# The recurrence's coefficients between the filters, its tables by eight pairs, its matrices by four groups, and the sums of tiles later

## The chip, the cores and the metric

The kernel runs on one core of a Trainium2 chip. The metric is the device time of one execution in microseconds (us). The core has TensorE (PE, with its weight loads shown apart as PEld), VectorE (DVE), ScalarE (ACT), GpSimd (POOL) and SyncE (SP), each with a queue of its own that is worked off in order, and 16 DMA engines.

## The reference

One layer of an encoder on two batches, a prompt of 1024 tokens and a sample of 256, with the same weights, all in float32:

```
x <- LN1(alpha*x + 0.5*SwiGLU_1(x))
x <- LN2(alpha*x + W_out[ RMS(S5(x)) ; RMS(Hyena(x)) ])
x <- LN3(alpha*x + 0.5*SwiGLU_2(x))
SwiGLU(x) = (silu(x @ w_gate) * (x @ w_up)) @ w_down       # 1024 -> 2816 -> 1024
S5:    ar, ai, bbr, bbi = discretize(lam, log_step, b)     # per direction, group and state
       h[l] = a * h[l-1] + bb u[l];  y = Re(c h) + d u     # 32 groups of 16 channels, 64 states, both directions
Hyena: k_f = rfft(filter);  z = gates[o] * (irfft(rfft(z) * k_f[o]) + bias[o] * z)
```

S5's coefficients depend on weights alone, as do Hyena's filters and their spectra. The kernel works them out at run time, beside the first SwiGLU.

## The kernel before, in words

**Precision.** Large products run as three products of float32 halves that PE takes in one pass: a helper `split` (L169 to L172) makes the high part on ACT (L171) and the low part on DVE (L172).

**Memory.** `Ctx.new` hands out buffers from 25 pieces of 2048 words per partition; a freed piece goes to the end of the list and is handed out again, and whoever writes it first waits until its last readers are through.

**Order.** The program is written by Python generators. `weave((gen, n), ...)` (L1567) always advances the generator whose yields so far, divided by its number n, are the smallest. The framework writes each engine's order when the program is built: what was emitted earlier has the higher priority, `high_priority(offset=...)` shifts it, and an instruction whose inputs are not expected yet is passed over. On the chip every engine then keeps that order.

**Stages.** The line of the weave tells what runs together:

- 0 to 527 us: `ffn` for four tiles (two of the sample, two of the prompt; 512 tokens) with `filter_spectra`, the filters of the sample and then of the prompt (L1722). Gate and up products are L298, down products L331. The weight loads of L281 and L314 are issued on SP shortly ahead of use.
- 527 to 1141 us: `ffn1_halves` for the prompt's other six tiles with `prep`, that is `s5_prep` and then `s5_mats` (L1723).
- then the in-projection with the scan (`s5`), which reads `scr["mat"]` and `scr["tab"]`; then Hyena with the sample's rest; from about 1925 us on the prompt's second SwiGLU.

**The six-tile SwiGLU.** `Blocks` holds seven operands made from x (two halves of the tokens, two halves of the features): "11", "21", "22" are blocks, "t1" to "t4" sums of blocks. `even` makes the first two, `odd` the others, with four subtractions on POOL (L1301), transposes on PE (L1308) and splits. `GateUp` makes seven operands of the weights, four of them sums (`sums`, L1363, on POOL in this SwiGLU, on DVE in the last one) which are split on ACT and DVE. `gated` then goes through 22 steps of 128 columns; each step has seven products of 12 matmuls (L1388), sums on DVE out of PSUM (L1409), a copy on ACT at its first product (L1421) and one store. `Down` (L1496) adds up the down products (L1541).

**The recurrence.** `s5_prep` (L432) works out the coefficients: some 130 DVE instructions on small tiles, most of them one after the other, thirteen PE instructions (nine transposes and products) and two Sin on ACT, with the loads of b (L507 to L509). It leaves `b23` (2 x 64 x 16 words per partition) and `tn` (7 x 2 x 32) in SBUF for `s5_mats` (L541). That makes tables first: for four pairs at a time seven levels of `cmul` (L421, six DVE instructions), each twice as wide as the last one, then copies on ACT and eight DMAs issued by ACT (L567) into `scr["tab"]`. Then the matrices: for two groups at a time six DVE products and sums (TT of L546), two transposes, two matmuls (L626) and two stores on SP.

The weaves and the buffers of the tables are

```
    weave((fa, 33), (filter_spectra((4, 5, 6, 7)), 155))
    weave((fb, 30), (prep((6, 7)), 165))
    ...
    c_, s_, n_, tm = K.ring(2, 4, 160), K.ring(2, 4, 160), K.ring(1, 4, 160), K.ring(1, 4, 64)
```

## Time and profile before

| | |
|---|---|
| median of 3 runs | 2615.12 us (2611.82 to 2616.24) |
| the profiled execution | 2612.26 us, its span 2610.5 us |
| instructions in the span | 32833 |
| PE busy | 2499.4 us (96%), 12605 matmuls |
| DVE busy | 1934.4 us (74%) |
| ACT, POOL busy | 865.8 us (33%), 213.3 us (8%) |
| mean granted PE clock | 0.987 |

Busy time is the time in which an engine had an instruction in work. Matmuls are pipelined and overlap, so a busy PE may still run below its rate; the number of matmuls in a stretch and the granted clock tell more. "Idle before" is what an engine stood still ahead of an instruction, with the engine and line that ended the wait. A line can be a helper's: L171 and L172 are all splits, L424 to L429 all of `cmul`.

### The profile page before, as it was taken

The page shows a single profiled execution, that of the slowest core. Times are in us where ns is not written, and L with a number is a line of the kernel's source. Part 1 is how long each engine was busy: PE and PEld are TensorE (multiplying, and loading weights), DVE is VectorE, ACT ScalarE, POOL GpSimd, SP SyncE. Part 2 cuts the span into 40 slices and gives each one's busy share as a digit, 9 for nine tenths or more (in the row PEclk, how much of TensorE's full clock was granted, in tenths as well). Part 3 has the DMA queues.
Part 4 walks back from the last instruction along what each step waited for, and adds up shares of the span by engine and source line. Part 5 has one row for each costly group of instructions (what it writes and reads, how often), then busy time and mean ns, then how long its engine had stood idle before and what let it go on. Part 6 is the DMA issues. An engine that isn't in the chain of part 4 may idle for free.

```text
span 2610.5 us, 32833 instructions
## 1 busy us (share of the span) xinstructions
PE 2499.4 (96%) x12605; PEld 2124.7 (81%) x12605; DVE 1934.4 (74%) x3153; ACT 865.8 (33%) x1315; POOL 213.3 (8%) x158
## 2 busy tenths in 40 slices
PE   8999999978989899999999999999989999999998
PEld 6777788878879888888888878999768888888887
DVE  6777777598997887466896978798886656556437
ACT  5443443333334342123444413333332222223200
POOL 0000000243233200010000000000230000000001
PEclk9999999989999999999999999999989999999999
DMA  6322332452545475355556654565332322235311
GB/s 196 118 88 85 100 107 89 137 130 68 148 144 141 138 234 154 92 163 146 158 171 190 222 204 147 161 194 154 121 130 89 93 77 82 88 131 200 118 44 65
DMA packets 359156, 346.90 MB, mean 133 GB/s; under 512 B 42220, under 2 KB 309125, under 8 KB 358230
## 3 DMA queue, kind: packets, MB, share of 16 engines
q1 hardware_dynamic: 323446, 326.44, 39.9%
q10 hardware_dynamic: 35552, 18.36, 2.6%
q8 instruction: 99, 1.62, 0.3%
q14 instruction: 59, 0.48, 0.1%
HBM read 261.37 MB, written 83.11 MB: 132 GB/s over the span
## 4 chain that ended last, share of the span: by engine, by line
PE 68%; DVE 20%; DMA 4%; issue 3%; POOL 2%; ACT 2%; SPq 0%; ACTq 0%; DVEq 0%; POOLq 0%
PE banks L1388 19%; PE banks L1541 14%; PE banks L298 12%; PE banks L331 5%; DVE s L172 4%; PE banks L860 4%; DVE s L930 3%; PE banks L777 3%; PE banks L1242 3%; PE banks L1064 2%; POOL s L1363 1%; ACT s L171 1%; DVE s L245 1%; DMA s<-in_ffn_w_gate_dram 1%; DVE s L1409 1%
## 5 line engine op out<-in xcount | busy, mean ns | idle before, releaser
L1388 PE MATMUL banks<-s,s 128*128 128x512 f32 (+1 forms) x3500 | 768.7, 371 | 26.2 <-DVE s L1409 17.0
L171 ACT ACTIVATE s<-s 128x1024 fp32r<-128x1024 f32 (+4 forms) x533 | 478.9, 915 | 845.5 <-PE banks L1541 132.9
L1388 PEld LDWEIGHTS banks<-s,s 128*128 128x128 f32 x3500 | 647.0, 191 | 106.4 <-DVE s L1409 19.2
L172 DVE TENSOR_TENSOR s<-s,s 128x1024 fp32r<-128x1024 f32 (+4 forms) x533 | 570.1, 1081 | 181.4 <-ACT s L171 170.0
L298 PE MATMUL banks<-s,s 128*128 128x512 f32 (+1 forms) x2112 | 400.5, 342 | 2.4 <-ACT s L171 1.2
L1541 PE MATMUL banks<-s,s 128*128 128x512 f32 x1232 | 386.8, 392 | 0.1
L298 PEld LDWEIGHTS banks<-s,s 128*128 128x128 f32 x2112 | 325.4, 191 | 53.0 <-issue 10.3
L1541 PEld LDWEIGHTS banks<-s,s 128*128 128x128 f32 x1232 | 230.4, 188 | 46.6 <-DVE s L172 0.6
L1541 PE MATMUL banks<-s 128*128 128x512 f32 x616 | 241.2, 392 | 0.0
L860 PE MATMUL banks<-s,s 128*128 128x512 f32 (+1 forms) x1152 | 237.6, 360 | 0.0
L1409 DVE TENSOR_TENSOR s<-banks,s 128x384 f32<-128x384 f32 (+1 forms) x220 | 136.0, 618 | 111.9 <-PE banks L1388 110.9
L860 PEld LDWEIGHTS banks<-s,s 128*128 128x128 f32 x1152 | 188.3, 189 | 28.2 <-DVE s L172 0.4
L331 PE MATMUL banks<-s,s 128*128 128x512 f32 x792 | 200.8, 396 | 4.1 <-ACT s L171 2.3
L1547 DVE TENSOR_TENSOR s<-banks,s 128x512 f32<-128x512 f32 x140 | 95.8, 688 | 134.3 <-PE banks L1541 134.2
L230 POOL TENSOR_TENSOR cst<-cst 128x1 f32<-128x1 f32 (+2 forms) x38 | 47.8, 1258 | 1618.0 <-DVE cst L229 1618.0
L331 PEld LDWEIGHTS banks<-s,s 128*128 128x128 f32 x792 | 144.9, 188 | 35.7 <-ACT s L171 2.7
L1541 PEld LDWEIGHTS banks<-s 128*128 128x128 f32 x616 | 115.8, 188 | 22.7
L1242 PE MATMUL banks<-s,s 128*128 128x512 f32 x480 | 124.7, 407 | 4.1 <-ACT s L171 1.6
L1242 PEld LDWEIGHTS banks<-s,s 128*128 128x128 f32 x480 | 89.3, 190 | 23.4 <-ACT s L171 2.0
L679 DVE TENSOR_TENSOR s<-banks,s 128x512 f32<-128x512 f32 (+2 forms) x112 | 59.1, 550 | 44.5 <-ACT s L796 20.4
L171 ACT ACTIVATE s<-banks 128x512 fp32r<-128x512 f32 x81 | 46.8, 596 | 131.1 <-PE banks L221 68.0
L777 PE MATMUL banks<-s,s 128*128 128x256 f32 x624 | 89.7, 285 | 0.0
(218 smaller groups left out, 2634.9 us busy)
## 6 DMA issues: line engine op xcount, KB each, us to landing
s<-in_ffn_w_gate_dram SPq DMA_DIRECT2D x88, 512.0 KB
s<-in_ffn_w_up_dram SPq DMA_DIRECT2D x88, 512.0 KB
s<-in_ffn_w_down_dram SPq DMA_DIRECT2D x88, 512.0 KB
scr_h<-s SPq DMA_DIRECT2D x22, 512.0 KB
s<-scr_h SPq DMA_DIRECT2D x22, 512.0 KB
scr_tab<-s ACTq DMA_DIRECT2D x64, 160.0 KB
s<-scr_mat SPq DMA_DIRECT2D x16, 640.0 KB
s<-scr_tab SPq DMA_DIRECT2D x16, 640.0 KB
```

The costliest lines, as they stand in the source:

```text
L171: K.nc.scalar.activation(out=hi, in_=src, func=AF.Copy)
L172: K.nc.vector.tensor_tensor(out=lo, in0=src, in1=hi.bitcast(F32), op=ALU.subtract)
L298: nc.tensor.matmul(pss[-1][c], lhsT=w[:, wv, d], rhs=xT.parts[k][c].at(d), start=(d == 0 and wv == 0 and k == 0), stop=(d == 7 and wv == 1))
L331: nc.tensor.matmul(ps, lhsT=h[s // 4][:, a, s % 4 * 128:(s % 4 + 1) * 128], rhs=w[:, b, dh * 512:(dh + 1) * 512], start=(n == 0), stop=(n ...
L777: nc.tensor.matmul(ps, lhsT=F[kt][a].v[:, s, i], rhs=b.v[:, s], start=(n == 0), stop=(n == 3 * NT // R - 1))
L860: nc.tensor.matmul(p, lhsT=w[:, wv, d], rhs=xT[nm].parts[k][c].at(d), start=(d == 0 and wv == 0 and k == 0), stop=(d == 7 and wv == 1))
L930: TT = lambda o, a, b, op: V.tensor_tensor(out=o, in0=a, in1=b, op=op)
L1242: nc.tensor.matmul(ps, lhsT=y[s // per][a].v[:, k, ts], rhs=W[k].v[:, b, dh * 512:dh * 512 + 512], start=(k == 0 and a == 0 and b == 0), s ...
L1388: self.K.nc.tensor.matmul(ps, lhsT=w[i][:, d], rhs=x[k][:, d], start=first and m == 0, stop=m == len(todo) - 1, skip_group_check=True)
L1409: TT = lambda o, a, b: V.tensor_tensor(out=o, in0=a, in1=b, op=ALU.add)
L1541: nc.tensor.matmul(ps, lhsT=p[a].v[:, o:o + 128], rhs=p[b].v[:, dh * 512:dh * 512 + 512], start=m == 0, stop=m == len(todo) - 1)
L1547: nc.vector.tensor_tensor(out=xv, in0=ps, in1=xv, op=ALU.add)
```

## The change

- `filter_spectra` runs the sample's filters, then `s5_prep`, then the prompt's filters. `s5_prep` stores its two results in DRAM (`scr["b"]`, `scr["turn"]`), and `s5_mats` loads them again.
- `s5_mats` makes the tables for eight pairs at a time with one set of buffers, and yields after every level; the matrices for four groups at a time.
- `Blocks` gets its buffers in two goes. `ffn1_halves` makes all even blocks first, and the four sums of the first weights and all odd blocks in `begin`, behind the first two products. Of the down weights two instead of three loads are issued ahead.
- `gated` issues the first product of step 1 ahead of the sixth of step 0, in both SwiGLUs that use it; the four buffers for c1, u2, u3 become two for c1 and one each for u2 and u3.
- The weaves' numbers change.

```diff
@@ s5_prep
-    keep.update(b=b23, turn=tn)
+    for k, b in (("b", b23), ("turn", tn)):
+        nc.sync.dma_start(out=keep[k], in_=b.v)
+        b.free()
     yield 4
@@ s5_mats
-    er, ei = keep["turn"].v[:, :, 0], keep["turn"].v[:, :, 1]
-    c_, s_, n_, tm = K.ring(2, 4, 160), K.ring(2, 4, 160), K.ring(1, 4, 160), K.ring(1, 4, 64)
-    for j in range(0, 32, 4):
+    turn, bs = K.new(7, 2, 32), K.new(2, 64, 16)
+    nc.sync.dma_start(out=turn.v, in_=keep["turn"])
+    nc.sync.dma_start(out=bs.v, in_=keep["b"])
+    er, ei = turn.v[:, :, 0], turn.v[:, :, 1]
+    c_, s_, n_, tm = (K.ring(1, 8, n) for n in (160, 160, 160, 64))
+    for j in range(0, 32, 8):
         d, q = divmod(j, 16)
...
             cmul(K, c[:, :, n:2 * n], s[:, :, n:2 * n], c[:, :, 0:n], s[:, :, 0:n],
-                 bc(er[:, lev, j:j + 4], 2, n), bc(ei[:, lev, j:j + 4], 2, n), t[:, :, 0:n])
+                 bc(er[:, lev, j:j + 8], 2, n), bc(ei[:, lev, j:j + 8], 2, n), t[:, :, 0:n])
+            yield 1.5
...
-                nc.scalar.dma_start(out=scr["tab"][half * 64:half * 64 + 64, q:q + 4, v, gg, d], in_=src[gg * 64:gg * 64 + 64])
-        yield 7
+                nc.scalar.dma_start(out=scr["tab"][half * 64:half * 64 + 64, q:q + 8, v, gg, d], in_=src[gg * 64:gg * 64 + 64])
+        yield 1.5
...
-    inj, injt = K.ring(1, 2, 8, 16), K.ring(2, 2, 128)
-    outm, tmp = K.ring(1, 2, 9, 16), K.ring(1, 2, 9, 16)
+    inj, injt = K.ring(1, 4, 8, 16), K.ring(2, 4, 128)
+    outm, tmp = K.ring(1, 4, 9, 16), K.ring(1, 4, 9, 16)
...
-            for q in range(0, 8, 2):
+            for q in range(0, 8, 4):
...
-                yield 2
+                yield 4
@@ Blocks
-        self.b = {n: (K.newr(4, self.width), K.newr(4, self.width)) for n in self.NAMES}
+        self.b = {}
         self.tmp = K.ring(1, 4, 512) if tmp else None
+
+    def make(self, names):
+        for n in names:
+            self.b[n] = self.K.newr(4, self.width), self.K.newr(4, self.width)
@@ gated
-    tmp, hb = K.ring(4, T), K.ring(1, 2, T)
+    cr, tmp, hb = K.ring(2, T), K.new(2, T), K.ring(1, 2, T)
...
     G.parts(1)
+    p1(1)
     p6(0)
...
-        if ft < END:
+        if 0 < ft < END:
             p1(ft + 1)
@@ emit
     def filter_spectra(ids):
         FC = filt_consts(K, A)
-        for nm in NAMES[::-1]:
-            yield from filters(K, A, nm, FC, scr, ids, {})
+        yield from filters(K, A, "sample", FC, scr, ids, {})
+        yield from s5_prep(K, A, scr, Banks(K, ids[-2:]))
+        yield from filters(K, A, "prompt", FC, scr, ids, {})
...
         X = Blocks(K, N // 2, False)
-        for j in range(N // 2):
-            x = K.new(2, D)
+        X.make(X.NAMES[0:2])
+        xs = [K.new(2, D) for _ in range(N // 2)]
+        for j, x in enumerate(xs):
             for i in range(2):
                 nc.sync.dma_start(out=x.v[:, i], in_=src[:, first + 2 * j + i])
             X.even(x.v, j, tb)
-            if j < N // 2 - 1:
-                X.odd(x.v, j, tb)
-                x.free()
         G = GateUp(K, g("ffn1_w_gate"), g("ffn1_w_up"), True)
         G.load()
         yield 0.01
         G.parts(0)
-        G.sums(0, 0)
-        G.sums(0, 1)
+        X.make(X.NAMES[2:])
         G.load()
 
         def begin():
-            X.odd(x.v, N // 2 - 1, tb)
-            x.free()
+            G.sums(0, 0)
+            G.sums(0, 1)
+            for j, x in enumerate(xs):
+                X.odd(x.v, j, tb)
+                x.free()
...
-            if n in (1, 2, 5):
+            if n in (1, 2):
                 dn.load()
...
-    weave((fa, 33), (filter_spectra((4, 5, 6, 7)), 155))
-    weave((fb, 30), (prep((6, 7)), 165))
+    weave((fa, 33), (filter_spectra((4, 5, 6, 7)), 183))
+    weave((fb, 33), (s5_mats(K, A, scr, scr, dict(prep=(6, 7))), 115))
```

## Rows read from the trace of the kernel before

**Rows 1.** The page's first part: busy us (share) xinstructions of each engine.

```profile
PE 2499.4 (96%) x12605; PEld 2124.7 (81%) x12605; DVE 1934.4 (74%) x3153; ACT 865.8 (33%) x1315; POOL 213.3 (8%) x158
```

**Rows 2.** Stretches: us; busy of PE, PEld, DVE, ACT, POOL; PEclk, DMA share, GB/s.

```profile
30.00:467.00 437.00, 429.00 (x2099) 339.04 (x2098) 329.97 (x465) 191.35 (x235) 0.00 (x0) 1.00 0.33 105
467.00:527.00 60.00, 59.99 (x296) 49.10 (x295) 37.96 (x56) 21.22 (x32) 16.12 (x12) 1.00 0.44 145
527.00:560.00 33.00, 23.27 (x116) 20.84 (x115) 31.87 (x56) 12.02 (x22) 21.04 (x14) 0.90 0.68 193
560.00:640.00 80.00, 71.31 (x380) 68.99 (x379) 69.09 (x181) 25.28 (x55) 22.37 (x16) 0.91 0.24 58
640.00:796.00 156.00, 134.95 (x719) 130.79 (x717) 147.00 (x477) 52.48 (x108) 47.51 (x34) 0.95 0.51 145
796.00:829.00 33.00, 30.39 (x173) 30.00 (x174) 19.58 (x34) 12.47 (x25) 14.03 (x10) 1.00 0.56 151
829.00:935.00 106.00, 96.38 (x576) 91.92 (x575) 92.06 (x169) 42.30 (x93) 24.84 (x18) 1.00 0.51 155
935.00:1141.00 206.00, 204.33 (x981) 168.09 (x980) 153.47 (x250) 52.44 (x74) 7.54 (x5) 1.00 0.49 151
1436.00:1951.00 515.00, 492.78 (x2744) 428.10 (x2743) 432.57 (x591) 167.97 (x262) 46.84 (x36) 0.98 0.52 169
1951.00:2360.00 409.00, 408.87 (x1803) 337.51 (x1802) 245.18 (x323) 118.06 (x150) 0.00 (x0) 1.00 0.31 99
```

**Rows 3.** Groups by line, 527 to 935 (busy, mean ns | idle before, releasers).

```profile
L1388 PE MATMUL banks<-s,s 128*128 128x384 f32 x1634 | 339.6, 347 | 22.5 <-DVE s L1409 17.0 <-DVE s L172 5.5
...
L172 DVE TENSOR_TENSOR s<-s,s 128x512 fp32r<-128x512 f32 x156 | 126.9, 829 | 26.8 <-ACT s L171 26.2
```

**Rows 4.** Timeline of PE, 553 to 576: start, us, what [idle before].

```profile
556.65 8.10 PE L1388 MATMUL banks<-s,s 128*128 128x384 f32 x45 [1.72 <-DVE s L1409]
...
574.67 1.65 PE L1388 MATMUL banks<-s,s 128*128 128x384 f32 x4 [3.67 <-DVE s L1409]
```

**Rows 5.** Waits, 527 to 935: who for whom, us in total, times, longest.

```profile
POOL s L1363 <- DVE s L172: 202.0, 35, 15.0
ACT s L171 <- POOL s L1363: 109.2, 51, 5.6
```

**Rows 6.** Line L1421, 790 to 835: ns min/median/max, first and last start.

```profile
L1421 ACT COPY s<-banks x3: 461/463/468, 796.4 to 829.5; 128x384 f32<-128x384 f32 x3
```

**Rows 7.** Busy us of DVE on line L546 alone, by stretch.

```profile
527.00:935.00 408.00, 50.43 (x94) 0.95 0.47 135
935.00:1050.00 115.00, 41.41 (x103) 1.00 0.58 182
```

**Rows 8.** Busy us by stretch while the loads of b run.

```profile
575.00:580.00 5.00, 5.00 (x17) 5.00 (x17) 4.95 (x24) 0.63 (x1) 0.42 (x1) 0.50 0.80 93
```

**Rows 9.** Groups of DVE by line and shape, 640 to 796.

```profile
L426 DVE TENSOR_TENSOR s<-s,s 128x4 f32<-128x4 f32 x8 | 4.5, 558 | 0.2
...
L425 DVE TENSOR_TENSOR s<-s,s 128x256 f32<-128x256 f32 x8 | 3.3, 416 | 0.0
...
L425 DVE TENSOR_TENSOR s<-s,s 128x128 f32<-128x128 f32 x8 | 2.3, 283 | 0.0
```

**Rows 10.** Timeline of DVE: two short instructions in a row.

```profile
594.17 0.21 DVE L424 TENSOR_TENSOR cst<-cst 128x64 f32<-128x64 f32 x1
594.30 0.21 DVE L425 TENSOR_TENSOR s<-cst 128x64 f32<-128x64 f32 x1
```

**Rows 11.** Line L567, all of it: ns min/median/max, first and last start.

```profile
L567 ACTq DMA_DIRECT2D scr_tab<-s x64: 582/637/1577, 654.5 to 804.4; - x64
```

**Rows 12.** Timeline of PE at the start of the last SwiGLU.

```profile
1937.49 2.92 PE L1388 MATMUL banks<-s,s 128*128 128x512 f32 x6 [2.26 <-DVE s L172]
```

**Rows 13.** The page's third part: ACT's DMA queue (packets, MB, share).

```profile
q10 hardware_dynamic: 35552, 18.36, 2.6%
```

**Rows 14.** Line L546, all of it: what DVE waited for (us, times).

```profile
  DMA scr_mat<-s: 1.2, 2
```

More of the change, by code (lines that the diff above doesn't have):

```diff
@@ L566, in s5_mats @@
             for gg in range(2):
-                nc.scalar.dma_start(out=scr["tab"][half * 64:half * 64 + 64, q:q + 4, v, gg, d], in_=src[gg * 64:gg * 64 + 64])
-        yield 7
-    for r in (c_, s_, n_, tm, keep["turn"]):
+                nc.scalar.dma_start(out=scr["tab"][half * 64:half * 64 + 64, q:q + 8, v, gg, d], in_=src[gg * 64:gg * 64 + 64])
+        yield 1.5
+    for r in (c_, s_, n_, tm, turn):
         r.free()
     banks, bank1 = Banks(K, cfg["prep"][:-1]), Banks(K, cfg["prep"][-1:])
-    bb, bb1 = keep["b"].v[:, 0], keep["b"].v[:, 1]
+    bb, bb1 = bs.v[:, 0], bs.v[:, 1]
     pwr, pwi = K.pw[:, 0], K.pw[:, 1]
     cin, cst, gw = K.ring(2, 2, 2, 64), K.ring(1, 2, 8, 16), K.ring(2, 15, 16)
-    inj, injt = K.ring(1, 2, 8, 16), K.ring(2, 2, 128)
-    outm, tmp = K.ring(1, 2, 9, 16), K.ring(1, 2, 9, 16)
+    inj, injt = K.ring(1, 4, 8, 16), K.ring(2, 4, 128)
+    outm, tmp = K.ring(1, 4, 9, 16), K.ring(1, 4, 9, 16)
     nc.sync.dma_start(out=K.dcol, in_=g("ssm_d").rearrange("(b g) h -> (g h) b", b=4))
@@ L595, in s5_mats @@
             kp = bank1.get(8, 16)
-            for q in range(0, 8, 2):
+            for q in range(0, 8, 4):
                 dg, gg = d * 32 + b * 8 + q, b * 8 + q
                 def powers(lo, hi, rev):
-                    r, i = (p[:, lo:hi, dg:dg + 2] for p in (pwr, pwi))
+                    r, i = (p[:, lo:hi, dg:dg + 4] for p in (pwr, pwi))
                     if rev:
@@ L606, in s5_mats @@
                 r, i = powers(0, 8, d == 0)
-                TT(iv, bc(bb[:, dg:dg + 2], 2, 8), r, ALU.mult)
-                TT(tv, bc(bb1[:, dg:dg + 2], 2, 8), i, ALU.mult)
+                TT(iv, bc(bb[:, dg:dg + 4], 2, 8), r, ALU.mult)
+                TT(tv, bc(bb1[:, dg:dg + 4], 2, 8), i, ALU.mult)
                 TT(iv, iv, tv, ALU.add)
                 it = injt.get()
-                ps = banks.get(2, 128)
+                ps = banks.get(4, 128)
                 with K.tc.high_priority(offset=-50):
-                    for j in range(2):
+                    for j in range(4):
                         nc.tensor.transpose(ps[:, j], iv[:, j].rearrange("p a b -> p (a b)"), K.ident)
                 nc.scalar.copy(out=it, in_=ps)
-                nc.sync.dma_start(out=scr["mat"][:, gg:gg + 2, d], in_=it)
+                nc.sync.dma_start(out=scr["mat"][:, gg:gg + 4, d], in_=it)
                 ov, tv = outm.get(), tmp.get()
                 r, i = powers(0, 9, d == 1)
-                TT(ov, bc(cs_[:, 0, q:q + 2], 2, 9), r, ALU.mult)
-                TT(tv, bc(cs_[:, 1, q:q + 2], 2, 9), i, ALU.mult)
+                TT(ov, bc(cs_[:, 0, q:q + 4], 2, 9), r, ALU.mult)
+                TT(tv, bc(cs_[:, 1, q:q + 4], 2, 9), i, ALU.mult)
                 TT(ov, ov, tv, ALU.add)
-                nc.sync.dma_start(out=scr["mat"][:, gg:gg + 2, 2 + d], in_=ov[:, :, 1 - d:9 - d].rearrange("p g t h -> p g (t h)"))
+                nc.sync.dma_start(out=scr["mat"][:, gg:gg + 4, 2 + d], in_=ov[:, :, 1 - d:9 - d].rearrange("p g t h -> p g (t h)"))
                 with K.tc.high_priority(offset=-100):
-                    for j in range(2):
+                    for j in range(4):
                         nc.tensor.matmul(kp[:, q + j], lhsT=ov[:, j, d:d + 8].rearrange("p t h -> p (t h)"), rhs=bb[:, dg + j],
                                          start=True, stop=True)
-                yield 2
+                yield 4
             nc.scalar.copy(out=K.kev, in_=kp.rearrange("p a b -> p (a b)"))
@@ L641, in s5_mats @@
                               in_=gv[:, 7 - s:15 - s].rearrange("p t h -> p (t h)"))
-    for r in (cin, cst, gw, inj, injt, outm, tmp, keep["b"]):
+    for r in (cin, cst, gw, inj, injt, outm, tmp, bs):
         r.free()
@@ L1418, in p1 @@
     def p1(ft):
-        st[ft] = s = {"ps": [K.ps[:, b * 512:b * 512 + T] for b in ids[ft % 2]], "c1": tmp.get()}
+        st[ft] = s = {"ps": [K.ps[:, b * 512:b * 512 + T] for b in ids[ft % 2]], "c1": cr.get()}
         product(ft, 1, 0, True)
@@ L1431, in p6 @@
         product(ft, 6, 1, True)
-        s["u2"] = tmp.get()
+        s["u2"] = tmp.v[:, 0]
         TT(s["u2"], s["ps"][1], s["c1"])
@@ L1440, in p7 @@
         product(ft, 7, 1, False)
-        s["u3"] = tmp.get()
+        s["u3"] = tmp.v[:, 1]
         TT(s["u3"], s["ps"][1], s["c1"])
@@ L1491, in gated @@
             yield 0.6
-    for r in [tmp, hb] + G.sv:
+    for r in [cr, tmp, hb] + G.sv:
         r.free()
@@ L1642, in filter_spectra @@
         FC = filt_consts(K, A)
-        for nm in NAMES[::-1]:
-            yield from filters(K, A, nm, FC, scr, ids, {})
-    keep, out, x1T = {}, {}, {}
+        yield from filters(K, A, "sample", FC, scr, ids, {})
+        yield from s5_prep(K, A, scr, Banks(K, ids[-2:]))
+        yield from filters(K, A, "prompt", FC, scr, ids, {})
+    out, x1T = {}, {}
     gi = mix_in(K, A, x1T, out, scr, dict(win=((0, 1, 2), (3,)), wtr=(4,)))
-    def prep(ids):
-        yield from s5_prep(K, A, keep, Banks(K, ids))
-        yield from s5_mats(K, A, keep, scr, dict(prep=ids))
     def to_mix():
@@ L1852, in prompt @@
                             X = Blocks(K, 4, True)
+                            X.make(X.NAMES)
                         turn(j - 1)
```

2 lines of the change are left out of this document (1 added, 1 removed).

## The prediction

> **What bounds the kernel now.** I read the page's first lines, then the busy times by stretch, then the groups of lines and the waits of the one stretch that stands out. The page says PE 96% busy and would leave nothing to gain [rows 1]. The stretches say otherwise [rows 2]. In 1951 to 2360, the last SwiGLU, PE has no idle time and DVE is at 60%. In 30 to 467, the first SwiGLU woven with the filters, PE idles 8.0 of 437 us with DVE at 75.5%. In 527 to 935, the gate and up products of six tiles woven with the whole preparation of the recurrence, PE is busy 356.3 of 408 us (the five stretches from 527 on), so 51.7 idle, and its clock is granted at 0.90, 0.91 and 0.95 in the first three, which is 3.3 + 7.2 + 7.8 = 18.3 us more: 70 us lost, 17%. DVE is busy there 359.6 of 408, 88%. The same rows give a scale of DVE share against PE idle: 75.5% with 1.8%, 84.0% with 4.3% (1436 to 1951), 86.8% with 9.1%, 94.2% with 13.5%.
>
> The groups show how DVE reaches PE: PE waits mostly for the sums of L1409 [rows 3], single waits up to 3.67 us [rows 4]. A second loop runs beside it: POOL's sums wait 202 us for DVE's splits, and ACT's splits 109 us for POOL [rows 5]. At full clock 45 products in a row take 8.10 us [rows 4], some 0.175 us each, so one of the 22 steps (84 products) needs 14.7 us of PE, 323 for all and about 328 with the small matmuls, against 408.
>
> **Part 1, the coefficients move between the filters.** The stretch 796 to 829 holds exactly two steps (L1421 opens each; it comes at both ends and once between [rows 6]) and none of the preparation's arithmetic: DVE 19.6 us, so 9.8 a step, 215 for 22. The other 145 us of the 360 are 50 of L546 [rows 7], in 640 to 796 some 57 of tables (147 less 9.2 steps of 9.8), 3 more of them ahead of 640, and so about 35 for the coefficients. These 35 leave. In the stage from 30 on POOL does nothing; without it I take 28 us (25 to 34, the present size). There DVE has 330 of 437; with 28 more the share nears 82%, and by the scale the PE idle share goes from 1.8 to about 3.7%: 429 / 0.963 = 445.5, **+8.5 us**. The weave stretches the filters from 28.1 to 28.9 of 33 units, so part falls into 467 to 527, where DVE is at 63%.
>
> The step's other instructions move too. While b is loaded (L507, L508) the DMA engines are 80% busy for only 93 GB/s [rows 8]. Beside them now stand the SwiGLU's weight loads on SP, which are needed soon after they land, at a DMA share of 0.33. Cost 0 to 10 us (the 10 us of the busy stretch); I take 3, as those engines have room. The 13 PE instructions and two Sin calls: 1.5. The two new stores on SP wait for the last operation of the step, and the weight loads issued after them wait behind; that is within the same 0 to 10. The two loads back, 1.2 MB, take some 8 us at 145 GB/s; the first cmul waits for them, the first two steps' weights have been issued before: 0 (0 to 3). Stage one together: **+13 us** (3 to 40).
>
> **Part 2, tables by eight pairs.** 336 cmul instructions become 168 of twice the width. A 128-element one takes 283 ns, a 256-element one 416 [rows 9], so 128 elements cost 133 and 150 ns are fixed; of two in a row the second starts 0.13 us after the first, which lasts 0.21 [rows 10], so 70 to 150 ns of each removed one are really saved: 12 to 25 us, I take 18. The width of 512 has a near row: L172 at 829 ns mean with POOL's sums beside it [rows 3].
>
> The SBUF lock speaks against longer instructions. One group of 128x4 instructions has a mean of 558 ns, twice that of a 128x128 group [rows 9], where POOL is busy 47.5 of 156 us [rows 2]. The Trainium skill ("SBUF — State Buffer", Who interferes with whom) says that a VectorE operation with two SBUF inputs and a GpSimd operation exclude each other for a whole instruction. By that rule fewer instructions meet POOL, but POOL stands behind each for longer; the rows bear out the first half, and no row here shows the second apart.
>
> If POOL's 88 sums each waited 0.27 us more (150 + 4 x 133 = 682 instead of 416 ns), it would be 23 us of an engine that is busy 30% of this stretch (124 of 408); half of that on the path is 12, none is 0. I take 0 and keep 12 for the range.
>
> **Part 3, matrices by four groups.** 192 products and sums become 96; 92 us over the whole (50 in the stretch, 41 behind it [rows 7]) less 7 to 14, so 81. Where they fall changes: the tables take 48 of 115 units against 33, 13.8 steps, and the matrices 18.4 more, of which 8.2, 45%, lie within the 22 steps (before 58%). 37 us instead of 50: 13 saved. In 935 to 1141 there are then 44 instead of 41 on a DVE that is 74% busy under a PE that idles 1.7 us: 0 (-1 to +3). The 40 copies and DMA issues of 0.64 us [rows 11] fewer are ACT's, which is under half busy.
>
> **Part 4, sums later.** At the start POOL has 12 subtractions of the odd blocks and 4 sums. Now ten of the subtractions are over by 527 (POOL 16.1 in 467 to 527), and PE idles 9.7 of the next 33 us. If all wait for the start, the sixth product needs 15 POOL operations of 1.4 us, 21 us, over which PE has three products (6.3) and 84 transposes (9): 6 us worse. If POOL starts early, as now, the third product fills 2.1 us and the tail is lighter: 6 better. I take 0, inside the next sum. In the last SwiGLU the same product (12 matmuls of 0.227, by 409 us for 1803 in its stretch [rows 2]; 2.7 us) moves into a gap where PE waits 2.26 us [rows 12]: **-2** (-4 to +2). One weight load fewer ahead of the down products: a row of 36 products lasts 9.4 us (206 / 22) and its 0.9 MB land in 6 at 151 GB/s, so two ahead are enough: 0 (to +6, once).
>
> **The sum.** DVE from 527 on: 360 - 35 - 18 - 13 = 294. At 82% that is 358 us, 30 over PE's 328. By the scale about 4% idle (14 us), and the rest for the clock after waits and for small gaps, which now take 28 of the 80. So 408 becomes 358, **-50**; 16 us a step and 6 for the start. Bounds: -75 when PE has its 328 and 5, -25 when steps stay near 17. Together -50 + 13 - 2 = -39 on the profiled execution's 2612.3: 2573. That execution lies 2.8 below the median of the runs, 2615.1, so the forecast is 2576.
>
> **Rivals.** (A) *One set of tables.* c and s have one buffer each instead of two, so DVE's memset at L553 waits until the set before has landed, and DVE works in order: L1409 and PE stand behind it. Price: eight issues of 0.64 us, 5, and 2.6 MB; ACT's queue moved 18.36 MB in 2.6% of the span [rows 13], 9.7 us for a set alone, 19 if half the engines are taken; 7 us pass anyway (1.5 of 115 units at 16 us a step). 9 to 18, three times, say 41: 2576 + 41 = **2617**. It decides if the built order puts the memset before the landing. Against it: the single buffer of -s and of the matrices exists already, and DVE waited 1.2 us in all for the matrices' stores [rows 14]. (B) *Slower: stage one becomes what the second is.* The filters' arithmetic gets denser (160 units in 28.9 instead of 132 in 28.1) and DVE's order there has PE's matmuls behind it. If 30 to 467 loses the 17% that 527 to 935 lost, 429 / 0.83 = 517, +80 in place of +13: 2576 + 67 = **2643**. It decides from a loss of 11%, where 429 / 0.89 = 482 is 45 us more and eats the gain; on the scale that is a DVE share near 90%, and I get 82. (C) *The loop and not DVE's load.* In 796 to 829 DVE is at 59%, and PE still idles 7.9%: split, sum, split, sum depend on each other across three engines. If steps stay at 17.5 the gain is 15: 2615 - 15 + 13 - 2 = **2611**.
>
> **How the numbers follow.** Forecast 0.72 (2545 to 2604), A 0.09, B 0.11, C 0.08. What can be told from no change is 0.2%, 5 us. Faster: 0.72 and a third of A and of C, 0.78. Same: the rest of A and C, nearly, 0.09. Slower: B and a little of A and C, 0.13. The range goes from the forecast's best end with a lighter start, 2540, to A, 2617; B lies outside.
>
> **What would show it.** From 527 on: DVE 290 to 300 us, clock back at 1.00, steps of about 16 us, 168 cmul lines the widest of 0.68 us. From 30 to 467: L436 and L507 in it, PE idle under 20 us. DVE waiting at L553 for scr_tab would be A; a DVE share of 90% before 467, B; DVE below 80% with steps of 17.5, C. I am wrong if stage one gives back over 40, or if DVE's relief leaves the waits at L1409 as long as they are.

## The result, and the profile of the changed kernel

The changed kernel takes 2594.4 us (median, 2592.7 to 2595.0) against 2614.3, a ratio of 0.9923 (95% interval 0.9906 to 0.9940). The forecast was 2576: the sign is right, and half of the expected 39 us came. The profiled execution has a span of 2592.3 us.

The page's first part, as [rows 1]: DVE has 34 us and 280 instructions (the page's x counts) less, PE's share is unchanged.

```profile
PE 2494.5 (96%) x12605; PEld 2123.9 (82%) x12605; DVE 1900.4 (73%) x2873; ACT 870.3 (34%) x1291; POOL 213.2 (8%) x158
```

Stretches of the changed kernel, with the columns of [rows 2]: first the fixed one up to 467, then cut at its own events: stage one up to the first gate product (532.8; before 527.2), the start up to the product that opens step 2 (586.9; before 572.3), the 20 steady steps up to the first down product (921.6; before 935.4), start and steps together, the down part.

```profile
30.00:467.00 437.00, 428.12 (x2053) 335.06 (x2052) 344.24 (x580) 193.23 (x242) 0.00 (x0) 0.99 0.36 108
...
30.00:532.80 502.80, 490.00 (x2361) 386.92 (x2360) 390.07 (x644) 212.24 (x269) 12.60 (x9) 0.99 0.37 113
532.80:586.90 54.10, 42.48 (x229) 38.26 (x227) 47.05 (x91) 22.09 (x42) 26.91 (x20) 0.91 0.34 109
586.90:921.60 334.70, 310.49 (x1745) 304.93 (x1744) 255.37 (x461) 125.58 (x238) 107.15 (x76) 0.97 0.50 143
532.80:921.60 388.80, 352.97 (x1973) 343.20 (x1971) 302.42 (x551) 147.68 (x278) 134.06 (x95) 0.96 0.48 138
921.60:1128.30 206.70, 205.58 (x995) 170.11 (x994) 152.73 (x204) 53.22 (x66) 5.12 (x4) 1.00 0.50 158
```

The same cuts of the kernel before:

```profile
30.00:527.20 497.20, 489.19 (x2394) 388.32 (x2393) 368.13 (x521) 212.57 (x267) 16.15 (x13) 1.00 0.35 110
527.20:572.30 45.10, 34.07 (x177) 31.34 (x175) 43.70 (x95) 16.41 (x31) 24.17 (x17) 0.92 0.53 151
572.30:935.40 363.10, 322.44 (x1782) 311.43 (x1783) 316.10 (x818) 128.29 (x268) 105.60 (x76) 0.96 0.47 133
527.20:935.40 408.20, 356.51 (x1959) 342.77 (x1958) 359.79 (x912) 144.70 (x298) 129.76 (x92) 0.95 0.47 135
```

So the steps gave 28.4 us (18.16 to 16.74 each), the start took 9.0 (4.4 of them are 40 transposes that moved there from stage one), stage one took 5.6 in this profile. The two spans differ by 18.2 us; 4.6 of them lie between the down part and the last SwiGLU, where I had forecast nothing and where the profiles of the experiments spread over 4 us. DVE's work in start and steps fell by 57.4 us, as intended, to 302 (forecast 294). What did not follow is the time: I had it at DVE / 0.82, but the share fell with the load, from 88% to 77.8%. For 57 us of DVE the stretch gave 19.4.

Groups and waits of 532.8 to 921.6, to be held against [rows 3] and [rows 5]; the line numbers are shifted by ten (L1388 is L1398, L1409 is L1419, L1363 is L1373):

```profile
L1398 PE MATMUL banks<-s,s 128*128 128x384 f32 x1668 | 338.9, 346 | 15.7 <-DVE s L1419 15.6
...
L172 DVE TENSOR_TENSOR s<-s,s 128x512 fp32r<-128x512 f32 x152 | 125.9, 837 | 43.0 <-ACT s L171 37.3 <-PE banks L632 4.2
...
L1398 PE MATMUL banks<-s 128*128 128x384 f32 x156 | 55.2, 354 | 11.8 <-DVE s L1419 11.7
```

```profile
POOL s L1373 <- DVE s L172: 183.1, 36, 12.1
ACT s L171 <- POOL s L1373: 105.0, 53, 4.6
```

Where the 28 us of the steps came from, counted from one of PE's starts to the next, over the 0.173 us that most take: waits of over 0.25 us for the matrices' arithmetic (L546, 9.6 us before) and for splits (L172, 4.9) are gone, and smaller excesses fell from some 25 to some 18. Not all of these are gaps: 76 matmuls before and 58 now start 0.3 to 0.4 us before the next one, with the granted clock at 0.96 and 0.97 on the mean; in no_prep_math below, at 1.00, there is one. PE's waits for the sums are as they were, 24.9 us before and 24.5 now, though DVE has a sixth less to do and is idle for 86 us of the stretch. An engine that is idle a fifth of the time and yet comes late may have something in its way at certain moments, and that is what the experiments look for.

### The profile page after: what moved, and what is told of

Same layout as the page of the kernel before. It is cut to its first block, busy times and chain, and to the rows that moved or that the text cites. A ratio compares the mean times of both kernels' runs of the same rounds, so it can differ in the third digit from the quotient of the medians.

```text
span 2592.3 us, 32411 instructions
## 1 busy us (share of the span) xinstructions
PE 2494.5 (96%) x12605; PEld 2123.9 (82%) x12605; DVE 1900.4 (73%) x2873; ACT 870.3 (34%) x1291; POOL 213.2 (8%) x158
## 4 chain that ended last, share of the span: by engine, by line
PE 69%; DVE 17%; DMA 5%; issue 3%; ACT 2%; POOL 2%; SPq 1%; ACTq 0%; DVEq 0%; POOLq 0%
PE banks L1398 24%; PE banks L1552 14%; PE banks L298 9%; PE banks L331 5%; DVE s L172 4%; PE banks L866 3%; DVE s L936 3%; PE banks L783 3%; PE banks L1248 2%; PE banks L1070 2%; ACT s L171 2%; POOL s L1373 1%; DVE s L751 1%; DMA s<-in_ffn_w_up_dram 1%; DMA s<-in_ffn_w_gate_dram 1%
## 5 line engine op out<-in xcount | busy, mean ns | idle before, releaser
L1398 PE MATMUL banks<-s,s 128*128 128x512 f32 (+1 forms) x3536 | 767.5, 369 | 19.4 <-DVE s L1419 15.6
L1398 PEld LDWEIGHTS banks<-s,s 128*128 128x128 f32 x3536 | 651.7, 191 | 97.6 <-DVE s L1419 15.6
L172 DVE TENSOR_TENSOR s<-s,s 128x1024 fp32r<-128x1024 f32 (+4 forms) x533 | 575.1, 1089 | 198.6 <-ACT s L171 187.0
L298 PEld LDWEIGHTS banks<-s,s 128*128 128x128 f32 x2112 | 324.8, 191 | 53.6 <-issue 9.2
L1552 PEld LDWEIGHTS banks<-s,s 128*128 128x128 f32 x1232 | 230.4, 188 | 47.8 <-DVE s L172 0.4
L1419 DVE TENSOR_TENSOR s<-banks,s 128x384 f32<-128x384 f32 (+1 forms) x220 | 136.6, 621 | 139.0 <-PE banks L1398 137.5
L866 PEld LDWEIGHTS banks<-s,s 128*128 128x128 f32 x1152 | 188.0, 189 | 28.0 <-DVE s L172 0.4
L331 PEld LDWEIGHTS banks<-s,s 128*128 128x128 f32 x792 | 146.7, 190 | 35.2 <-issue 1.9
L1248 PEld LDWEIGHTS banks<-s,s 128*128 128x128 f32 x480 | 89.3, 191 | 23.4 <-DVE s L1170 2.0
L783 PEld LDWEIGHTS banks<-s,s 128*128 128x128 f32 x624 | 81.0, 190 | 7.1 <-ACT s L171 2.5
```

Of the source, the lines that this page charges most:

```text
L172: K.nc.vector.tensor_tensor(out=lo, in0=src, in1=hi.bitcast(F32), op=ALU.subtract)
L298: nc.tensor.matmul(pss[-1][c], lhsT=w[:, wv, d], rhs=xT.parts[k][c].at(d), start=(d == 0 and wv == 0 and k == 0), stop=(d == 7 and wv == 1))
L331: nc.tensor.matmul(ps, lhsT=h[s // 4][:, a, s % 4 * 128:(s % 4 + 1) * 128], rhs=w[:, b, dh * 512:(dh + 1) * 512], start=(n == 0), stop=(n ...
L783: nc.tensor.matmul(ps, lhsT=F[kt][a].v[:, s, i], rhs=b.v[:, s], start=(n == 0), stop=(n == 3 * NT // R - 1))
L866: nc.tensor.matmul(p, lhsT=w[:, wv, d], rhs=xT[nm].parts[k][c].at(d), start=(d == 0 and wv == 0 and k == 0), stop=(d == 7 and wv == 1))
L1248: nc.tensor.matmul(ps, lhsT=y[s // per][a].v[:, k, ts], rhs=W[k].v[:, b, dh * 512:dh * 512 + 512], start=(k == 0 and a == 0 and b == 0), s ...
```

## The experiments

Each run is of the changed kernel with one edit, unless it says otherwise. "Stretch" is from the first gate product to the first down product, "step" the mean of the 20 steady ones, both from the run's profile. Ratios are to the kernel before, measured in the same job.

| kernel | median us | ratio (95% interval) | stretch us | DVE in it | step us |
|---|---|---|---|---|---|
| before | 2614.3 | 1 | 408.2 | 359.8 | 18.16 |
| changed | 2594.4 | 0.9923 (0.9906 to 0.9940) | 388.8 | 302.4 | 16.74 |
| narrow | 2599.0 | 0.9948 (0.9929 to 0.9968) | 396.0 | 329.0 | 16.94 |
| coeff_late | 2609.2 | 0.9979 (0.9967 to 0.9991) | 403.9 | 323.6 | 17.61 |
| early_sums | 2588.8 | 0.9911 (0.9891 to 0.9930) | 384.1 | 300.4 | 16.64 |
| no_prep_math | 2561.8 (one run) | | 360.7 | 227.5 | 15.58 |
| sums_first | 2584.3 | 0.9895 (0.9873 to 0.9916) | 383.6 | 306.0 | 16.45 |
| four_sv | 2598.2 | 0.9944 (0.9925 to 0.9963) | 399.8 | 302.0 | 17.04 |
| sums_dve | 2566.5 | 0.9824 (0.9806 to 0.9842) | 367.6 | 306.4 | 15.99 |
| no_pool_sums | 2553.5 (one run) | | 356.2 | 259.3 | 15.27 |
| pool_detached | 2592.5 (one run) | | 391.4 | 316.6 | 16.62 |
| before_sums_dve | 2567.5 | 0.9824 (0.9807 to 0.9841) | 361.8 | 344.4 | 16.17 |
| dve_first | 2558.8 | 0.9794 (0.9775 to 0.9814) | 360.2 | 305.7 | 15.60 |
| dve_first_early | 2559.7 | 0.9798 (0.9779 to 0.9816) | 359.3 | 299.8 | 16.04 |

### The parts, one undone at a time

**narrow**: parts 2 and 3 undone.

```diff
-    for j in range(0, 32, 8):
+    for j in range(0, 32, 4):
...
-        c, s, t = c_.get(), s_.get(), tm.get()
+        h = j % 8
+        c, s, t = (r.get()[:, h:h + 4] for r in (c_, s_, tm))
...
-            for q in range(0, 8, 4):
+            for q in range(0, 8, 2):
```

> The changed kernel with parts 2 and 3 undone: tables by four pairs (two halves of the same buffers in turn, one yield of 6 per set) and matrices by two groups; the coefficients stay between the filters, the sums stay late. Theory (VectorE's load): the arithmetic of the preparation is 31 us of DVE longer, most of it within the 22 steps, so the steady steps go from 16.7 to about 17.7 us and the time from 2594 to some 2610 (2605 to 2620). Rival (bursts): what PE waits for is the length of a single burst ahead of the sums, and shorter instructions make up for more of them: 2590 to 2598. Rival (the loop sets the step): steps stay at 16.7, time 2594 plus or minus 3.

DVE got 26.6 us more in the stretch, the stretch 7.2, the time about 5 to 7 (ratio 0.9948 against 0.9923; the intervals overlap). The first theory's 16 us didn't come. Parts 2 and 3 did to DVE what I forecast, 27 against 31, and it was worth a quarter of that.

**coeff_late**: part 1 undone.

```diff
-        yield from filters(K, A, "sample", FC, scr, ids, {})
-        yield from s5_prep(K, A, scr, Banks(K, ids[-2:]))
-        yield from filters(K, A, "prompt", FC, scr, ids, {})
+        for nm in NAMES[::-1]:
+            yield from filters(K, A, nm, FC, scr, ids, {})
...
+    def prep(ids):
+        yield from s5_prep(K, A, keep, Banks(K, ids))
+        yield from s5_mats(K, A, keep, scr, dict(prep=ids))
```

> The changed kernel with part 1 undone: the coefficients are worked out again at the start of the second stage and kept in SBUF, with the pace of the weave such that the matrices end at the same place. Theory: the first stage gives back 6 to 10 us, and the second gets 35 us of DVE work, which at 78 to 88% busy is some 35 to 42 us; 2594 + 25 to 35 = 2620 to 2630. Rival (part 1 is worth little, because the start of the second stage waits for GpSimd's subtractions in any case): the coefficients fit beside them, 2590 to 2600.

The time is 15 us more, with intervals apart: below what the theory said, above the rival. Most of what the change brings is this part. In stage one DVE has 364.9 us against 390.1 (25 less; I had 28 for the step), in the stretch 21 more; of the matrices more is left for the down part, which takes 212.0 instead of 206.7.

Stage one itself is better read from all profiles than from one. Nine kernels (the changed one, narrow, no_prep_math, sums_first, four_sv, sums_dve, no_pool_sums, pool_detached, dve_first) have the same 2449 matmuls in the same order up to the first gate product. They reach it at 522.5 to 532.8, median 524.6, and the changed kernel's own profile is the slowest. 2.8 of its 8.2 us over no_prep_math arise ahead of 67 us, and 3.6 in one wait near its end and the matmuls just behind it. PE's timeline in the changed kernel with DVE's ahead of it, and then PE's in sums_dve, with the wait before each group in brackets:

```profile
503.42 4.02 DVE L172 TENSOR_TENSOR s<-s,s 128x512 fp32r<-128x512 f32 x3 [2.19 <-ACT s L171]
...
508.69 0.95 PE L1318 MATMUL banks<-cst,s 128*128 128x128 f32 x4 [3.92 <-DVE s L172]
```

```profile
500.64 0.66 PE L1318 MATMUL banks<-cst,s 128*128 128x128 f32 x4 [1.80 <-DVE s L172]
```

With 4.4 for the transposes that left, 524.6 stands for 529.0; the code of before reached this point at 527.2 and, in before_sums_dve, at 529.3. coeff_late, without the coefficients there, has 524.2. So they cost stage one 0 to 2 us by these and 5.6 in the one profile, at the low end of my 3 to 40 or below it. In the wait at 508 three splits in a row last 4.02 us, 1.34 each, beside two subtractions on GpSimd (503.33 to 506.29); a split of this size takes 0.685 with GpSimd at rest, as the runs on the port will show. Why the instructions meet so in one execution and not in another, and where the rest of the 10 us comes from, I can't say; a difference of a few us in one profile's stage is no finding.

**early_sums**: part 4's order at the start undone.

```diff
+            if j < N // 2 - 1:
+                X.odd(x.v, j, tb)
+                x.free()
...
         def begin():
-            G.sums(0, 0)
-            G.sums(0, 1)
-            for j, x in enumerate(xs):
-                X.odd(x.v, j, tb)
-                x.free()
+            X.odd(x.v, N // 2 - 1, tb)
+            x.free()
```

> The changed kernel with part 4's order at the start undone: the odd blocks and the first two sums come before the gate products as in the kernel before, all blocks made at once, the weight loads of the down part as before; p1(1) stays early. Theory (the late sums cost 9 us at the start, of which 4.4 are transposes that only moved): the start goes from 54.1 to about 46 us, stage one's end from 532.8 to about 537: 2590 (2588 to 2593). Rival (late sums are even: what the start gains the tail of stage one loses): 2594 plus or minus 2. Rival (they gain, because stage one's tail has 5 us less of waits): 2596 to 2602.

2588.8, as the first theory had it, but the two intervals overlap. The stretch is 4.7 us shorter, which is the 4.4 of the transposes; stage one, with these transposes back in it, ends at 527.2. So the order at the start is even to within these measurements, or a few us against the change: my 0 (-6 to +6) holds.

### Is it VectorE's load?

**no_prep_math**: the DVE arithmetic of tables and matrices is left out.

```diff
-            cmul(K, c[:, :, n:2 * n], s[:, :, n:2 * n], c[:, :, 0:n], s[:, :, 0:n],
-                 bc(er[:, lev, j:j + 8], 2, n), bc(ei[:, lev, j:j + 8], 2, n), t[:, :, 0:n])
...
-                TT(iv, bc(bb[:, dg:dg + 4], 2, 8), r, ALU.mult)
-                TT(tv, bc(bb1[:, dg:dg + 4], 2, 8), i, ALU.mult)
-                TT(iv, iv, tv, ALU.add)
```

> The changed kernel with VectorE's arithmetic of the tables and matrices left out (the buffers are filled once); every copy, transpose, DMA and yield stays. It shows the floor of a step. DVE has then some 9.8 us a step, under 65%. Theory (load): the steady steps fall from 16.7 to 14.8 to 15.3 us, the waits at the sums vanish, the time is about 2594 - 30 to 35 = 2560 to 2565. Rival (the loop of splits and sums over three engines): steps stay at 16.0 to 16.6, as in the stretch of the kernel before that held no such arithmetic and took 16.6 a step, and the time is 2585 to 2592.

The time, 2561.8, is what the load theory named; the step, 15.58, lies between the two. 75 us of DVE in the stretch are worth 28 us: 0.37 each, as the 57 of the change were worth 0.34. A relation holds, but a weak one, and at 62% DVE PE still loses 1 us a step to waits at the sums and smaller excesses over 0.173 us. While PE waits for the sums of L1419 in the changed kernel's steps (24.5 us in waits over 0.25), DVE works on splits for 11.4 us, on the preparation for 7.9 and on the sum itself for 7.2 (overlaps count twice). The splits weigh most.

### Order, loop or port

**sums_first**: the sums of the products are given priority where DVE's order is laid out.

```diff
-    TT = lambda o, a, b: V.tensor_tensor(out=o, in0=a, in1=b, op=ALU.add)
+    def TT(o, a, b):
+        with K.tc.high_priority(offset=60):
+            V.tensor_tensor(out=o, in0=a, in1=b, op=ALU.add)
```

> The changed kernel in which the sums of the gate and up products are given priority over whatever else VectorE has ready when its order is laid out. Of the 24.5 us that TensorE waits for these sums in the 20 steady steps, DVE spends 11.4 on splits and 7.9 on the preparation. Theory (order): with the sums ahead, some 10 to 15 of these 19 us go, steps from 16.7 to 16.0 to 16.3, time 2594 - 10 = 2584. Rival (the sums are first already when they become ready; what they meet is one instruction under way, which no order changes): steps 16.6 to 16.8, 2590 to 2597.

The time is the theory's, its reason is not: the waits at the sums are 23.2 us instead of 24.5, and steps of 16.45 lie between its 16.0 to 16.3 and the rival's 16.6 to 16.8. The steps gave 5.7 us, half of it in the excesses below 0.25 us, and this profile's stage one was 8.6 shorter, which the edit doesn't touch. A small gain, then, with an interval that overlaps the changed kernel's.

**four_sv**: four buffers for GpSimd's sums instead of two.

```diff
-        self.sv = self.sv or [K.new(4, 128) for _ in range(2)] if self.fine else self.sv or [K.new(2, 4, 128)]
+        self.sv = self.sv or [K.new(4, 128) for _ in range(4)] if self.fine else self.sv or [K.new(2, 4, 128)]
```

> The changed kernel with four buffers for GpSimd's sums instead of two, so that the second pair of sums need not wait for the splits of the first pair. Theory (the loop split, sum, split, sum sets what is left of the waits): POOL's 162 us of waiting for the splits fall by more than half and steps go to 16.0 to 16.2, time 2580 to 2584. Rival (the loop has slack; GpSimd's waits cost nothing): POOL waits elsewhere, steps 16.6 to 16.8, 2590 to 2597.

GpSimd's waits in the stretch of four_sv, as [rows 5]:

```profile
POOL s L1377 <- DMA s<-in_ffn_w_up_dram: 102.3, 11, 17.7
POOL s L1377 <- DVE s L172: 101.2, 14, 13.3
```

The wait for the splits fell from 183 to 101 us, and a wait of 102 us for the next weights took its place. The step became 17.04, no shorter, and the time is just above the rival's. That speaks against the loop, but not cleanly: this kernel has a new wait of ACT's, shown under pool_detached.

**sums_dve**: the 88 sums of the weights on VectorE.

```diff
-        eng = K.nc.gpsimd if self.fine else K.nc.vector
+        eng = K.nc.vector
```

> The changed kernel with the 88 sums of the weights on VectorE instead of GpSimd, so that GpSimd does nothing within the steps. A sum takes 1.2 to 1.4 us on GpSimd; the split of the same 512 elements takes 0.68 on VectorE alone and 1.37 beside GpSimd. Theory (VectorE's load, 0.37 us of time for each us of it): 80 sums of 0.68 us are 54 us more, the splits fall by 0.14 us each, 19 us; 35 net, steps from 16.7 to 17.4, time 2594 + 13 = 2607. Rival (the port: GpSimd's operations hold VectorE's splits): steps fall to 16.2 or less and the time to 2585. Rival (the loop over three engines): same direction, 2580 to 2588.

28 us faster than the changed kernel, 45 faster than before. DVE does 88 more operations of 0.68 us in start and steps, and is busy there for 306.4 us instead of 302.4: most of what it got in work it lost in lengthening, which is counted below. The load theory is wrong by sign. The port and the loop both named the direction, and both named less, 2580 to 2588. This edit can't part them, as it takes GpSimd out of both.

**no_pool_sums**: these sums are left out, the splits stay.

```diff
-            TT(s[0], u[:, 0:4], u[:, 4:8], ALU.add)
-            TT(s[1], s[0], g[:, 0:4], ALU.subtract)
+        elif ft == 0 and not second:
+            for v in s:
+                K.nc.vector.memset(v, 0.5)
```

> The changed kernel with GpSimd's sums of the weights left out (their buffers are filled once and split as before); VectorE's work is the same. It shows what GpSimd costs in all, by the port it shares and by the loop. Theory (half of TensorE's waits at the sums are splits that GpSimd lengthens): the splits fall from 820 to 680 ns, DVE by 19 us, steps to 16.2 to 16.4, time 2594 - 8 = 2586. Rival (GpSimd holds the loop): steps 15.6 or less, 2572. Rival (nothing): 2590 to 2597.

2553.5, 41 us below the changed kernel where I expected 8. The splits are at 686 ns, as forecast, but the steps of 15.27 lie below the theory's 16.2 to 16.4 and below what the loop's rival named. PE's waits at the sums fell from 24.5 to 4.2 us in the steps. Whether by the port or by the loop this run can't tell either.

**pool_detached**: GpSimd does the same sums into buffers that nobody reads.

```diff
-            TT(s[0], u[:, 0:4], u[:, 4:8], ALU.add)
-            TT(s[1], s[0], g[:, 0:4], ALU.subtract)
+            TT(v[0], u[:, 0:4], u[:, 4:8], ALU.add)
+            TT(v[1], v[0], g[:, 0:4], ALU.subtract)
```

> The changed kernel in which GpSimd does the same 88 sums into two buffers that nobody reads, while the splits read buffers that were filled once: GpSimd's work without its place in the loop. With GpSimd's sums left out altogether the steps took 15.27 us and VectorE 213 us instead of 255 in them. Theory (the port: a GpSimd operation and a VectorE operation with two SBUF inputs hold each other up): DVE's splits stay at 800 to 840 ns and the steps at 16.3 to 16.8 us, the time at 2580 to 2594. Rival (the loop: the splits wait for the sums): steps of 15.2 to 15.5, time 2553 to 2560. Half and half would be 15.9.

Without GpSimd's sums the step is 15.27; with them, though no split waits for them, it is 16.62, in the range of the port's theory. The waits behind this step are others, though. pool_detached has two further buffers, as four_sv has, and in both ACT waits far longer for the store of the step before, ahead of the silu (L1437; here L1443, in four_sv L1441). The changed kernel, pool_detached and four_sv, columns as in [rows 5]:

```profile
ACT s L1437 <- DMA scr_h<-s: 8.6, 5, 3.0
...
ACT s L1443 <- DMA scr_h<-s: 38.0, 15, 7.0
...
ACT s L1441 <- DMA scr_h<-s: 30.6, 8, 6.3
```

So the step of pool_detached doesn't settle it; the durations of single instructions do more. DVE by line and shape over the steady steps: the changed kernel, then no_pool_sums, then pool_detached (count | busy, mean ns of one).

```profile
L172 DVE TENSOR_TENSOR s<-s,s 128x512 fp32r<-128x512 f32 x134 | 108.4, 818 | 38.9 <-ACT s L171 33.3 <-PE banks L632 4.2
L1419 DVE TENSOR_TENSOR s<-banks,s 128x384 f32<-128x384 f32 x99 | 54.6, 552 | 29.4 <-PE banks L1398 28.7
...
L425 DVE TENSOR_TENSOR s<-s,s 128x32 f32<-128x32 f32 x3 | 2.6, 883 | 0.1
```

```profile
L172 DVE TENSOR_TENSOR s<-s,s 128x512 fp32r<-128x512 f32 x130 | 88.3, 686 | 38.2 <-ACT s L171 37.8
L1424 DVE TENSOR_TENSOR s<-banks,s 128x384 f32<-128x384 f32 x98 | 54.2, 553 | 38.5 <-PE banks L1403 38.2
```

```profile
L172 DVE TENSOR_TENSOR s<-s,s 128x512 fp32r<-128x512 f32 x131 | 108.7, 843 | 31.0 <-ACT s L171 26.1 <-PE banks L1404 4.8
```

Operations with both inputs in SBUF (s,s) take longer when GpSimd is at work; the sums of L1419, with one input in PSUM, the memory that PE's products are written to (banks), take 552 or 553 ns either way. Of the 166 splits of 512 elements in the changed kernel's stretch, the 118 that overlap no GpSimd operation take 685 ns and none of them over 800; the 48 that do take 1136 on the mean. The lengthening is a matter of single instructions. This is DVE, then GpSimd, then PE around two of PE's waits:

```profile
685.28 1.29 DVE L428 TENSOR_TENSOR s<-s,s 128x64 f32<-128x64 f32 x1
686.49 0.28 DVE L424 TENSOR_TENSOR s<-s,s 128x128 f32<-128x128 f32 x1
686.69 0.54 DVE L1419 TENSOR_TENSOR s<-banks,s 128x384 f32<-128x384 f32 x1
...
755.25 3.11 DVE L172 TENSOR_TENSOR s<-s,s 128x512 fp32r<-128x512 f32 x2 [1.85 <-ACT s L171]
758.28 0.68 DVE L428 TENSOR_TENSOR s<-s,s 128x512 f32<-128x512 f32 x1
758.88 0.55 DVE L1419 TENSOR_TENSOR s<-banks,s 128x384 f32<-128x384 f32 x1
...
684.71 1.78 POOL L1373 TENSOR_TENSOR s<-s 128x512 f32<-128x512 f32 x1 [1.70 <-DVE s L172]
...
754.63 1.29 POOL L1373 TENSOR_TENSOR s<-s 128x512 f32<-128x512 f32 x1
756.54 1.26 POOL L1373 TENSOR_TENSOR s<-s 128x512 f32<-128x512 f32 x1 [0.62 <-DVE s L172]
...
687.29 0.69 PE L1398 MATMUL banks<-s 128*128 128x384 f32 x1 [2.98 <-DVE s L1419]
...
759.48 0.44 PE L1398 MATMUL banks<-s 128*128 128x384 f32 x1 [3.22 <-DVE s L1419]
```

At 685.28 an operation on 64 elements, which takes 0.22 us elsewhere in the same answer, lasts 1.29, until GpSimd's sum ends at 686.49. At 755.25 two splits last 3.11 us instead of 1.4 beside two GpSimd sums. Each time the sum that PE waits for stands behind them in DVE's order. PE has one product, 12 matmuls or some 2.1 us, between handing a bank to DVE for its sum and needing it back; two held instructions use that up.

This agrees with the Trainium skill ("SBUF — State Buffer", Who interferes with whom): a VectorE instruction with two SBUF inputs and a GpSimd instruction that reads SBUF shut each other out for a whole instruction, and one with at most one SBUF input isn't touched, outside the modes in which VectorE uses both of its port pairs. All 61 instructions that are counted as lengthened in the changed kernel have two SBUF inputs.

How much it is in all: I took each DVE instruction's duration over the median of its line and shape in the runs without GpSimd's sums, where it is more than 60 ns over. That gives 61 us in 73 of 911 instructions for the kernel before, 49 us in 61 of 550 for the changed one, 58 for narrow, 31 for no_prep_math, 66 for pool_detached. Each of them overlaps a GpSimd operation. The sizes don't follow the stretches in the table: pool_detached has the most at 391 us, and four_sv has 49 at 400.

More telling is where they stand. For each of PE's waits of over 0.25 us at the sums in the steps I looked for lengthened instructions ahead of that sum in DVE's order, from 2.1 us before PE's last start on. In the changed kernel 12 of 13 waits have them, 23.1 of 24.5 us, and the lengthening alone covers 18.0; in the kernel before 8 of 12, 19.4 of 24.7 us, covering 15.0; in no_prep_math 11 of 12. In no_pool_sums, sums_dve and before_sums_dve none of three each has one. In pool_detached it is 2 of 10 and in four_sv 7 of 15, so these two steps are held in good part by something else, and neither run parts port and loop. The loop may have a share: ahead of five of the 13 waits DVE also stood idle for over 1.5 us, mostly for a split's high part from ACT. How large it is isn't shown.

### What the change is worth without it

**before_sums_dve**: the kernel before with the one line of sums_dve and nothing of the change.

```diff
-        eng = K.nc.gpsimd if self.fine else K.nc.vector
+        eng = K.nc.vector
```

> The kernel before, with the sums of the weights on VectorE instead of GpSimd, and nothing of the change. In the changed kernel the same edit took 28 us off (2594 to 2566). Theory (GpSimd's hold on VectorE took part of what the change should have brought: a load taken from DVE is worth more where nothing else lengthens the waits): the edit gives less here, as DVE is 87% busy and gets 54 us of sums for some 45 to 50 of lengthening that it loses: 2600 (2595 to 2608), so that the change is worth 34 us without GpSimd instead of 20. Rival (the two are independent): 2615 - 28 = 2587. Rival (DVE is the bound here, and the sums on it cost more than the port gave): 2620.

All three were wrong: 2567.5, 47 us below the kernel before and the same as sums_dve. Without GpSimd's sums the change is worth nothing in all (0.9824 and 0.9824): in the profiles its steps are 3.6 us shorter, stage one and the start together 3.6 longer. Its stretches, start and steps:

```profile
529.30:567.80 38.50, 33.08 (x181) 31.54 (x180) 37.00 (x84) 16.21 (x30) 5.90 (x4) 0.91 0.61 176
567.80:891.10 323.30, 311.31 (x1776) 300.29 (x1775) 307.35 (x914) 129.79 (x270) 0.00 (x0) 0.99 0.52 148
```

In the steps DVE is 95% busy, and PE idles 12.0 of 323.3 us at a clock of 0.99. In the kernel before DVE was 87% busy there and PE idled 40.7 of 363.1. So here a DVE that is nearly full serves PE well; in start and steps one of its 996 instructions is lengthened, against 73 of 911.

**dve_first** and **dve_first_early**: sums_dve with the edit of sums_first, and the same with that of early_sums.

```diff
-        eng = K.nc.gpsimd if self.fine else K.nc.vector
+        eng = K.nc.vector
...
+        with K.tc.high_priority(offset=60):
+            V.tensor_tensor(out=o, in0=a, in1=b, op=ALU.add)
```

> The changed kernel with the sums of the weights on VectorE and the sums of the products given priority in VectorE's order. Alone the first gave 2566 (steps 15.99), the second 2584 (steps 16.45). Theory (order still counts where waits for sums are left): those waits are 6.7 us in the 20 steps, so at most 5 more: 2562. Rival (no more): 2566 plus or minus 3.

> As the run before it, and with the order of the kernel before at the start (the odd blocks and first sums ahead of the gate products), which alone gave 2589 beside 2594. Theory (the start is better with the sums early): 2558. Rival (with the sums on VectorE, which is 93% busy at the start, early or late is the same): 2562 to 2567.

2558.8 and 2559.7, below sums_dve, sums_first and early_sums, and 1.4% and 1.3% below the changed kernel. The first's steps are 15.60 against 15.99 of sums_dve; of the 7.7 us in the time, 3 are beyond the 5 I allowed, and the intervals still touch. The early start adds nothing beside 2558.8; its 2559.7 lies between the theory's 2558 and the rival's 2562 to 2567: start 38.5 instead of 48.2 with 4.4 of transposes moved, but steps of 16.04.

## Why the prediction was half right

**The bound.** I read the scale of DVE share against PE idle as cause and effect: 94.2% with 13.5% idle. before_sums_dve has 95% with 3.7%. The scale also left out 796 to 829, which my rival C names, with 59% and 7.9%. In [rows 2] all stretches with over 5% of PE idle have POOL busy for 23 to 64% of the time, and those with POOL under 10% idle at most 4.3%, whatever their DVE share. The column beside the one I read goes with the idle time better, though not alone: 467 to 527 has POOL at 27%, DVE at 63% and no idle time.

**The step that failed** is "At 82% that is 358 us", the -50 of the sum. DVE's 294 us was nearly right (302). Its share was not constant: the stretch measured 388.8, or 384.4 without the transposes that moved into it, so -24 in place of -50. My bounds of -75 to -25 just miss it. It is the mechanism that failed, not the size alone: with a sixth less to do DVE left the waits for its sums at 24.5 us (24.9), while single instructions were held by GpSimd. The time lies within my range of 2540 to 2617 because a gain of 20 us still falls into it, not because DVE's share set it; that it came to half of the forecast is no merit of the sum.

**The hold of the port**, which I priced at 0 with 12 kept for the range, lengthened DVE's instructions by 61 and 49 us in the two kernels, and the edit that puts the sums on VectorE took 47 and 28 us off the time. That edit removes the loop over three engines too, so the whole of it is not shown to be the port's. I asked only what the change would add to it, from the mean of one group of 558 ns [rows 9], and not what it already cost. The rows to see it were there: L172 at a mean of 829 ns [rows 3], where no instruction of its shape is over 0.8 us without a GpSimd operation beside it. The change gained what it did with GpSimd at work, and nothing without it; it takes 361 instructions out of GpSimd's way and 12 us out of the lengthening. That this is the whole of its gain is not shown: of the 14.5 us of waits for the matrices' arithmetic and for splits that it took away, 9.9 had no lengthened instruction ahead of them. What makes up its 20 us with GpSimd at work, and why they vanish without it, stays open.

**Part 1** was put at +13 for stage one; it was +5.6 in the profile and 0 to 2 by the nine. DVE reached 78.8% of 30 to 467 instead of 82, and PE's idle time there went from 8.0 to 8.9 us. The stage without POOL takes the work at little price. **Parts 2 and 3** took 27 us off DVE (31 forecast) and some 6 off the time. **Part 4** was 0 to within 6, as forecast; in the last SwiGLU the wait stands as it stood [rows 12], and its -2 came as less than 1:

```profile
1919.77 4.64 PE L1398 MATMUL banks<-s,s 128*128 128x512 f32 x10 [2.26 <-DVE s L172]
```

**The rivals.** (A) didn't happen; what DVE waited for the tables' landing in the stretch is 3.7 us instead of 41:

```profile
DVE s L558 <- DMA scr_tab<-s: 2.1, 1, 2.1
...
DVE s L427 <- DMA scr_tab<-s: 1.6, 1, 1.6
```

(B) didn't either: DVE 78%, stage one within 2%. (C) had the signs half right, DVE below 80% with waits that stay, at steps of 16.7 instead of 17.5, and the cause at most in part: the waits stand behind lengthened instructions, four_sv loosens the loop and gains nothing, but neither it nor pool_detached rules the loop out. My line "or if DVE's relief leaves the waits at L1409 as long as they are" named what happened.

## What to carry to other kernels

A high busy share is no bound by itself: look at the durations of one line and shape, and if they spread, at what another engine does in the long ones, before pricing the removal of work. Where GpSimd and VectorE both read SBUF beside a tight product loop, the first experiment is to move GpSimd's part to VectorE, one line here and worth more than the whole change. A stage's time from a single profile can be off by several us with the same instructions, so compare it over all profiles that share them.
